# Every second piece of weights with its 16-bit groups of matmuls first

## The chip, the core and the metric

One NeuronCore of a Trainium2 chip runs the whole kernel. The metric is the device time of one execution in microseconds (us). Before the change three executions took 2743.44, 2739.66 and 2746.03 us, median 2743.44. One more execution was recorded by the hardware profiler. TensorE appears as PE (matmuls) and PEld (weight loads), VectorE as DVE, ScalarE as ACT, GpSimd as POOL, SyncE as SP; an engine's name with a q (SPq) is its queue of DMA issues.

## What is computed

A decoder block for 512 tokens with a model width of 2048, all in float32. The input is normalised and multiplied by one wide matrix; its columns feed a linear recurrence with matrix state (16 heads of 64), a sliding-window attention and two sets of gates. Both branches are projected, gated, added, projected again and added to the input. A gated feed-forward part with a short convolution follows. Cut to the lines that carry matrix products:

```
h = rms_norm(x, norm1_g)
z = h @ w_in                                  # 2048 x 9152
o_rw  = rwkv7_mix(token_shift(z[...]), ...)   # recurrence over 512 tokens
o_att = swa_attention(q, k, v, ...)
x = x + (sigmoid(zg_r) * (o_rw @ w_branch[:1024]) + sigmoid(zg_a) * (o_att @ w_branch[1024:])) @ w_out
h = rms_norm(x, norm2_g)
u = h @ w_up                                  # 2048 x 11264
x = x + (silu(gate) * val) @ w_down           # conv over 3 tokens in between; 5632 x 2048
```

## The kernel before

**Products in three groups.** [...] Weights arrive by DMA in a tile `raw`. ACT writes `whi`, the value rounded to the engine's 32-bit matmul type (float32r); DVE then writes `wlo = raw - whi` in bfloat16. The activations exist as `hi` (float32r) and `lo` (bfloat16) in the same way. A *piece* is one such converted tile of weights, and PE runs three groups of matmuls on it, always in this order: group 0 is hi times hi in the 32-bit type, group 1 is the upper half of `whi`, read as bfloat16 by `top()`, with the low activations, group 2 is `wlo` with bfloat16 activations. All three add into the same PSUM banks. Group 0 and 1 need `whi` from ACT, group 2 needs `wlo` from DVE, so `wlo` may be as late as two groups after a piece has begun.

**Three places do this.** `project` (line 273) serves the input projection and the branch projections: a piece is 128x512 weights, a group is 4 matmuls of 512 columns, and weights are the stationary operand. `steps_of` (line 1046) serves `w_out` and `w_down`, as seven products on half-size blocks: a piece is 128x1024, a group is 4 matmuls of 512 columns with the activations stationary; two pieces (`q` = 0 and 1) share one tile of activations. `Block.mm` (line 1185) serves `w_up`, seven products a column block as well: a piece is 128x1024, a group is 8 matmuls of 256 columns.

**Buffers.** The converted tiles rotate: 4 of each of `whi` and `wlo` in `project` (pool `hl`), 3 in the other two places (pool `hlp`). A `whi` buffer comes free when group 1 of its piece has ended, a `wlo` buffer when group 2 has ended, `raw` when DVE has made `wlo`. ACT and DVE each work through their own instructions in a fixed order, so an instruction that waits for a buffer holds up what stands behind it.

**What sets the order.** A scheduler places the instructions of the first half (input projection, attention, recurrence) from its own estimate of times; the recurrence's matmuls stand among those of `project` at set places of the list `stream` (`behind`). In `w_up` the order is written out (`steps`, `prep`, `run`): conversions run two pieces ahead of the matmuls, and `pin` keeps them as written.

Of the kernel before, what the change touches and what calls it, by code (L numbers as in the profile page):

```python
# [135 lines left out]
def block_kernel(ctx: ExitStack, tc: tile.TileContext, d: Dims, a: dict, out: bass.AP):  # L136
    nc = tc.nc
    act, dve, pool, pe, sync = nc.scalar, nc.vector, nc.gpsimd, nc.tensor, nc.sync
# [54 lines left out]
    def rsqrt_small(pl, ss, scale, eps, mx=None, tag="rq"):  # L193
        n = ss.shape[-1]
        tl = [pl.tile([P, 8], F32, name=f"{tag}{i}", tag=f"{tag}{i}", bufs=2)[:, :n] for i in range(3)]
        v, y, t = tl
        if mx is not None:
            dve.tensor_scalar(v, ss, mx, None, op0=ALU.max)
        else:
            dve.tensor_scalar(v, ss, scale, eps, op0=ALU.mult, op1=ALU.add)  # L200
        dve.tensor_scalar(t.bitcast(I32), v.bitcast(I32), 1, None, op0=ALU.logical_shift_right)
        dve.tensor_scalar(y.bitcast(I32), t.bitcast(I32), -1, 0x5F3759DF, op0=ALU.mult, op1=ALU.add)
        dve.tensor_scalar(v, v, -0.5, None, op0=ALU.mult)
        for _ in range(3):
            dve.tensor_tensor(t, y, y, op=ALU.mult)
            dve.tensor_tensor(t, t, v, op=ALU.mult)
            dve.scalar_tensor_tensor(y, t, 1.5, y, op0=ALU.add, op1=ALU.mult)
        return y

    pin = tc.keep_in_program_order  # L210
# [9 lines left out]
    def quarter(w, src, c):  # L220
        return sum_d[w][src][c] if isinstance(src, str) else a["w_" + w][src[0], src[1], 2 * c : 2 * c + 2]
# [21 lines left out]
        return lambda: pool.dma_start(dst, second, accum_op=ALU.add, max_dma_last_dim=4096)  # L243

    stream = []

    def top(x):
        x = x.bitcast(BF16)
        return x[(slice(None),) * (len(x.shape) - 1) + (slice(1, None, 2),)]
# [5 lines left out]
    def load_w(src):  # L255
        nk, ncol = src.shape[1:]
        n = nk * ncol
        raw = wp["raw"].tile([P, 512], F32, name="raw", tag="raw")[:, :n].rearrange("p (k c) -> p k c", c=ncol)
        wp["last"] = sync.dma_start(raw, src)
        hi = wp["hl"].tile([P, 512], F32R, name="whi", tag="whi")[:, :n].rearrange("p (k c) -> p k c", c=ncol)  # L260
        lo = wp["hl"].tile([P, 512], BF16, name="wlo", tag="wlo")[:, :n].rearrange("p (k c) -> p k c", c=ncol)
        act.activation(hi, raw, AF.Copy)  # L262
        dve.tensor_tensor(lo, raw, hi.bitcast(F32), op=ALU.subtract)  # L263
        wp["n"] += 1
        if wp["n"] in wp["after"]:
            wp["after"].pop(wp["n"])()
        elif wp["step"] == 3 and wp["n"] <= HELD:
            pass
        elif wp["n"] % wp["step"] == 0 or wp["n"] in extra:
            sums_along()()  # L270
        return hi, lo

    def project(acc, src, xhi, xlo, x16=None, pre=()):
        nk = src.shape[1]
        for k0 in range(0, nk, 4):
            n = min(4, nk - k0)
            whi, wlo = pre[k0 // 4] if k0 // 4 < len(pre) else load_w(src[:, k0 : k0 + n])
            ops = [[(whi[:, j], xhi[:, k0 + j]) for j in range(n)],
                   [(top(whi[:, j]), xlo[:, k0 + j]) for j in range(n)],
                   [(wlo[:, j], x16[:, k0 + j] if x16 is not None else top(xhi[:, k0 + j])) for j in range(n)]]  # L280
            for i, part in enumerate(ops):
                for j, (l, r) in enumerate(part):
                    stream.append(pe.matmul(acc, l, r, start=k0 + i + j == 0, stop=k0 + n == nk and i == 2 and j == n - 1))  # L283


    id16 = cstp.tile([P, P], F16, name="id16")
# [8 lines left out]
    if True:  # L295
# [39 lines left out]
        def ztile(c0):  # L335
            acc = accp.tile([P, S], F32, name="acc", tag="acc")
            project(acc, zt[c0], xhi, xlo, x16 if scaled else None, first.pop(c0, ()))
            return acc
# [5 lines left out]
        r = rsqrt_small(p0, ssum, 1.0 / d.D, RMS_EPS)  # L344
        spread = []
        with tc.tile_pool(name="x0_ps", bufs=1, space=PSUM) as ps0:
            ps = ps0.tile([P, S], F32, name="ps_r")
# [55 lines left out]
        with ExitStack() as pt:  # L403
# [4 lines left out]
            def small():  # L408
                return mps.tile([P, S], F32, name="mi", tag="mi")
# [53 lines left out]
            for t in range(1, NKV):  # L463
                for c0, then in ((d.c_ka, keys), (d.c_va, values)):
                    acc = ztile(c0 + t * P)
# [25 lines left out]
            for g in range(NHK):  # L491
# [7 lines left out]
                for n in range(NT):  # L499
                    ts = slice(n * P, (n + 1) * P)  # L500
                    k0 = 0 if n else BLK
                    nk = 2 * BLK - k0
# [29 lines left out]
                    for kb in kbs:  # L532
                        ps = small().rearrange("p (h c) -> p h c", c=P)
# [3 lines left out]
                    ps = small()  # L537
                    for kb in kbs:
                        for i in range(2):
                            pe.matmul(ps, vhl[:, n - 1 + kb, g].rearrange("p e c -> p (e c)"),  # L540
                                      phl[i][:, kb].rearrange("p h c -> p (h c)"),
                                      start=kb == kbs[0] and i == 0, stop=kb == kbs[-1] and i == 1)
                    ol = ap_.tile([HD, S], F32, name="ol", tag="ol", bufs=2)
                    act.activation(ol, ps[HD:P], AF.Copy)
                    ps, ol = (x[0:HD].rearrange("p (e j c) -> p e j c", e=2, c=P) for x in (ps, ol))
# [5 lines left out]
        with ExitStack() as pr:  # L551
# [30 lines left out]
            acc = ztile(d.c_wd)  # L582
# [5 lines left out]
            acc = ztile(d.c_ad)  # L588
# [3 lines left out]
            for i in range(NG):  # L592
                acc = ztile(d.c_gd + i * P)
# [354 lines left out]
    KH = NK // 2  # L948
# [27 lines left out]
    with ExitStack() as pbb:  # L976
# [5 lines left out]
        order = [(m + e, i) for m in range(0, NK - 4, 2) for i in (0, 1) for e in range(2)]  # L982
        order += [(m, i) for i in (1, 0) for m in range(NK - 4, NK)]
        g = {}
        for m, i in order:
            hi, lo, r0, n, gi = parts[i]
# [9 lines left out]
            acc = accp.tile([P, S], F32, name="acc", tag="acc")  # L996
# [36 lines left out]
    def raw_tile(nm="raw", n=6):  # L1033
        return rwp.tile([P, WC], F32, name=nm, tag=nm, bufs=n)

    def banks(pl, nm):
        return [[pl.tile([P, S], F32, name=f"{nm}{t}{q}") for q in range(NQW)] for t in range(NT // 2)]

    def fetch(w, i, c, pl, pin=free):

        hhi, hlo = (pl.tile([P, 2, TH], t, name=f"h{e}", tag=f"h{e}") for e, t in (("hi", F32R), ("lo", BF16)))
        hr = pl.tile([P, 2, TH], F32, name="hraw", tag="hraw")
        pin(sync.dma_start(hr, right_d[w][c][RIGHT_AT[PRODUCTS[i][3]]]))
        return lambda: split(hhi, hlo, hr, pin), hhi, hlo

    def steps_of(w, i, acc, c, pl, got=None):

        _, start, src, _, _ = PRODUCTS[i]
        make, hhi, hlo = got or fetch(w, i, c, pl)
        if not got:  # L1050
            make()
        for q in range(2):
            wr = raw_tile()
            sync.dma_start(wr, quarter(w, src, c)[q])
            whi, wlo = (hlp.tile([P, WC], t, name=f"w{e}", tag=f"w{e}") for e, t in (("hi", F32R), ("lo", BF16)))
            act.activation(whi, wr, AF.Copy)  # L1056
            dve.tensor_tensor(wlo, wr, whi.bitcast(F32), op=ALU.subtract)  # L1057
            fst, lst = start and c + q == 0, c == NB[w] - 1 and q == 1
            for j in range(3):
                for t in range(NT // 2):  # L1060
                    ts = slice(t * P, (t + 1) * P)
                    for e in range(NQW):
                        dst, es = acc[t][e], slice(e * S, (e + 1) * S)
                        l, r = ((hhi[:, q, ts], whi[:, es]), (hlo[:, q, ts], top(whi[:, es])), (top(hhi[:, q, ts]), wlo[:, es]))[j]
                        pe.matmul(dst, l, r, start=fst and j == 0, stop=lst and j == 2, skip_group_check=True)  # L1065

    def taken_out(i, acc, xr, scale, done):
        ci, tj, sign = PRODUCTS[i][4]
# [86 lines left out]
    class Block:  # L1155
# [29 lines left out]
        def mm(self, n):  # L1185
            if n == "P1":
                x = ups.tile([P, S], F32, name="X", tag="X")
                self.X = x[:, :TH]
                self.Z = x[:, TH:] if self.f < NPRE else upy.tile([P, S], F32, name="Z", tag="Y")[:, :TH]
            if n == "P7":  # L1190
                self.Y = upy.tile([P, S], F32, name="Y", tag="Y")[:, :TH]
            into = {"P2": "Z", "P7": "Y", "Q4": "Y"}.get(n, "X")
            ps = getattr(self, "Z" if self.apart and n in ("P5", "P3") else into)
            start = n in ("P1", "P7") or n == "P2" and self.f >= NPRE or n == "P5" and self.apart
            whi, wlo = (x.rearrange("p (k c) -> p k c", c=P) for x in self.hl.pop(n))
            xh, xl = bq[{"P1": "b11", "P2": "b21", "P7": "t3", "P6": "t2", "P5": "t1", "Q4": "t4", "P3": "b22"}[n]]
            for i in range(3):
                for k in range(KH):
                    l, r = ((whi[:, k], xh[:, k]), (top(whi[:, k]), xl[:, k]), (wlo[:, k], top(xh[:, k])))[i]
                    pin(pe.matmul(ps, l, r, start=start and k + i == 0, stop=k == KH - 1 and i == 2, skip_group_check=True))  # L1200

        def out(self, n):
            if n == "P7":
# [74 lines left out]
    queue, order = [], {x: i for i, x in enumerate(steps)}  # L1278
# [65 lines left out]
    with tc.tile_pool(name="sqp", bufs=1, side="right", reuse_waits="tile") as sqp:  # L1344
        yx = ExitStack()
        py = yx.enter_context(tc.tile_pool(name="psY", bufs=1, space=PSUM, side="right", reuse_waits="tile"))
        acc = {"X": banks(px, "X"), "Y": banks(py, "Y")}
# [116 lines left out]
    with ExitStack() as pd:  # L1464
        pxy = pd.enter_context(tc.tile_pool(name="psD", bufs=1, space=PSUM, reuse_waits="tile"))
        acc = {n: banks(pxy, n) for n in "YX"}
# [94 lines left out]
```

## Time and profile before

| what | value |
|---|---|
| three executions | 2739.66 to 2746.03 us, median 2743.44 |
| the profiled execution | 2737.99 us, span of the core 2736.2 us |
| PE busy in the span | 2678.0 us |
| DVE, ACT, POOL busy | 1993.9, 1345.1, 231.3 us |
| granted TensorE clock | 0.999 |
| input projection, attention, recurrence | from 0 to about 1300 us |
| `w_out` | about 1300 to 1450 us |
| `w_up` | about 1448 to 2310 us |
| `w_down` | about 2300 to 2736 us |

The stages are told apart by the lines of the matmuls: line 283 is `project`, line 1065 `steps_of`, line 1200 `Block.mm`. In a row of the groups the columns are line, engine, operation, what is written and read, shapes, count, then busy time and the mean length of one in ns, then idle time before it and who ended that. In a row of the timeline they are start in us, length in us, engine, line, operation, operands and count; rows of neighbours of one kind are merged, so a row's length runs from the first one's start to the last one's end. Matmuls of a stream overlap in such rows: each record is longer than the distance to the next start.

### The profile page before, as it was taken

To read this page: it belongs to the slowest core of one execution; us is meant where nothing else is said; L and a number is where in the kernel's file an instruction comes from. 1 tells how busy PE (TensorE), PEld (TensorE's weight loads), DVE (VectorE), ACT (ScalarE), POOL (GpSimd) and SP (SyncE) were. 2 spreads that over 40 slices of the span, in tenths; PEclk is the share of its full clock that TensorE was granted. 3 is DMA by queue.
4 is the path that set the end of the run, shared out by engine and by line. 5 is a ranking of instruction groups with operands and counts; after the bars stand their busy time and mean duration, and the time that the engine had idled before them with its cause. 6 is when DMAs were issued, how large, how long until landed. Compare 5 with 4: busy or idle time off the path is not lost.

```text
span 2736.2 us, 45737 instructions
## 1 busy us (share of the span) xinstructions
PE 2678.0 (98%) x17227; PEld 1832.8 (67%) x17410; DVE 1993.9 (73%) x3476; ACT 1345.1 (49%) x2261; POOL 231.3 (8%) x308
## 2 busy tenths in 40 slices
PE   8999999999999999999999999999999999999999
PEld 4555566666666665555558889999999998555554
DVE  6787777877787775455678788888888888555655
ACT  6445445544544543322466555555555555444443
POOL 0001111111111001011000111101111110000000
PEclk9999999999999999999999999999999999999999
DMA  6557788779878767888785889888899888877775
GB/s 238 157 152 199 209 217 214 205 196 232 212 198 213 186 178 210 257 244 292 252 275 170 234 231 250 251 235 241 244 250 246 236 238 280 295 241 245 259 256 181
DMA packets 228333, 623.80 MB, mean 228 GB/s; under 512 B 24960, under 2 KB 45072, under 8 KB 227088
## 3 DMA queue, kind: packets, MB, share of 16 engines
q1 hardware_dynamic: 159552, 445.23, 49.4%
q0 software_dynamic: 37216, 136.33, 25.6%
q10 hardware_dynamic: 31344, 39.31, 4.1%
q8 instruction: 136, 2.23, 0.3%
q14 instruction: 85, 0.70, 0.1%
HBM read 571.16 MB, written 191.18 MB: 279 GB/s over the span
## 4 chain that ended last, share of the span: by engine, by line
PE 81%; DVE 10%; DMA 4%; ACT 2%; issue 2%; SPq 0%; DVEq 0%; ACTq 0%
PE acc L283 26%; PE X L1200 16%; PE X L1065 11%; PE Y L1065 9%; PE Y L1200 8%; PE Z L1200 4%; DVE wlo L263 2%; PE psS L833 1%; PE psG L824 1%; DMA rsb<-rsd 1%; DVE wlo L1183 1%; PE bulk L809 1%; DMA raw<-in_w_dn_dram 1%; DMA raw<-in_w_z_dram 1%; PE bulk L761 1%
## 5 line engine op out<-in xcount | busy, mean ns | idle before, releaser
L1057 DVE TENSOR_TENSOR wlo<-raw,whi 128x1024 bf16<-128x1024 f32 x210 | 256.7, 1225 | 192.2 <-ACT whi L1056 192.0
L283 PE MATMUL acc<-xhi,whi 128*128 128x512 f32 x1152 | 376.8, 441 | 10.9 <-ACT whi L262 10.4
L262 ACT ACTIVATE whi<-raw 128x512 fp32r<-128x512 f32 x352 | 220.1, 629 | 313.0 <-PE acc L283 251.3
L1056 ACT ACTIVATE whi<-raw 128x1024 fp32r<-128x1024 f32 x210 | 222.2, 1060 | 278.2 <-PE X L1065 146.3
L263 DVE TENSOR_TENSOR wlo<-raw,whi 128x512 bf16<-128x512 f32 x352 | 239.7, 688 | 97.7 <-ACT whi L262 59.9
L283 PE MATMUL acc<-xlo,whi 128*128 128x512 bf16 x1080 | 301.2, 383 | 4.0 <-issue 0.5
L283 PE MATMUL acc<-xlo,wlo 128*128 128x512 bf16 x1028 | 279.5, 379 | 2.1
L1183 DVE TENSOR_TENSOR wlo<-raw,whi 128x1024 bf16<-128x1024 f32 x184 | 224.8, 1223 | 72.5 <-ACT whi L1181 71.8
L1200 PEld LDWEIGHTS <-wlo 128*128 128x128 bf16 x2464 | 237.4, 96 | 39.5
L283 PEld LDWEIGHTS acc<-xhi,whi 128*128 128x128 f32 x1152 | 211.6, 190 | 65.2 <-ACT whi L262 11.5
L1181 ACT ACTIVATE whi<-a 128x1024 fp32r<-128x1024 f32 x124 | 131.0, 1056 | 228.3 <-DVE a L1176 209.8
L1200 PEld LDWEIGHTS <-whi 128*128 128x128 bf16 x2464 | 216.8, 98 | 34.7
L283 PEld LDWEIGHTS <-wlo 128*128 128x128 bf16 x1408 | 135.4, 98 | 150.3 <-issue 5.2
L283 PEld LDWEIGHTS <-whi 128*128 128x128 bf16 x1408 | 111.8, 100 | 159.4 <-issue 95.5
L1183 DVE TENSOR_TENSOR wlo<-a,whi 128x1024 bf16<-128x1024 f32 x124 | 152.0, 1225 | 64.2 <-ACT whi L1181 62.9
L1181 ACT ACTIVATE whi<-raw 128x1024 fp32r<-128x1024 f32 x184 | 192.4, 1047 | 3.3 <-PE X L1200 1.6
L1200 PE MATMUL X<-b,whi 128*128 128x256 f32 (+1 forms) x1472 | 192.1, 283 | 0.8 <-ACT whi L1181 0.3
L1200 PE MATMUL X<-t,whi 128*128 128x256 f32 (+1 forms) x1408 | 183.8, 283 | 3.2 <-ACT u L1227 2.5
L1200 PE MATMUL Y<-t,whi 128*128 128x256 f32 (+1 forms) x1408 | 183.8, 283 | 0.5 <-DVE u L1229 0.5
L1065 PE MATMUL X<-whi,hhi 128*128 128x512 f32 x480 | 153.3, 441 | 1.6 <-ACT whi L1056 1.6
L1065 PEld LDWEIGHTS <-hhi 128*128 128x128 bf16 x840 | 81.5, 97 | 103.7
L1251 DVE SCALAR_TENSOR_TENSOR c<-u,par,c 128x512 f32<-128x512 f32 x176 | 131.5, 747 | 14.1 <-ACT c L1248 13.9
(389 smaller groups left out, 4584.2 us busy)
## 6 DMA issues: line engine op xcount, KB each, us to landing
raw<-in_w_up_dram SPq DMA_DIRECT2D x170, 512.0 KB
raw<-in_w_z_dram SPq DMA_DIRECT2D x288, 256.0 KB
s_dn<-in_w_dn_dram POOLq DMA_DIRECT2D x88, 512.0 KB, 7.5
raw<-s_dn SPq DMA_DIRECT2D x88, 512.0 KB
raw<-in_w_up_dram POOLq DMA_DIRECT2D x80, 512.0 KB, 8.7
raw<-in_w_dn_dram SPq DMA_DIRECT2D x66, 512.0 KB
s_dn<-in_w_dn_dram SPq DMA_DIRECT2D x44, 512.0 KB
s_dn<-s_dn SPq DMA_DIRECT2D x44, 512.0 KB
```

The lines of the kernel that those rows point to most:

```text
L262: act.activation(hi, raw, AF.Copy)
L263: dve.tensor_tensor(lo, raw, hi.bitcast(F32), op=ALU.subtract)
L283: stream.append(pe.matmul(acc, l, r, start=k0 + i + j == 0, stop=k0 + n == nk and i == 2 and j == n - 1))
L761: ins = pe.matmul(ps[:, n], wt[:, 0, n], both(n), start=True, stop=False)
L809: pin(pe.transpose(ps[:, e, q], X[:, e, 2 * q : 2 * q + 2].rearrange("p n c -> p (n c)"), id16))
L1056: act.activation(whi, wr, AF.Copy)
L1057: dve.tensor_tensor(wlo, wr, whi.bitcast(F32), op=ALU.subtract)
L1065: pe.matmul(dst, l, r, start=fst and j == 0, stop=lst and j == 2, skip_group_check=True)
L1181: pin(act.activation(hi, t, AF.Copy))
L1183: return lambda: pin(dve.tensor_tensor(lo, t, hi.bitcast(F32), op=ALU.subtract))
L1200: pin(pe.matmul(ps, l, r, start=start and k + i == 0, stop=k == KH - 1 and i == 2, skip_group_check=True))
L1251: pin(dve.scalar_tensor_tensor(t, u[:, i, j + 1 : j + 1 + S], cw[:, j + 1, ci : ci + 1], t, op0=ALU.mult, op1=ALU.add))
```

## The change

A pair of orders, `turns`, is defined. Even pieces keep groups 0, 1, 2; odd pieces run 1, 2, 0. What counts as odd is the second and fourth piece of a projection in `project`, the piece `q` = 1 in `steps_of`, and every second step of the written order in `Block.mm`. [...] No instruction is added or taken away.

```diff
     stream = []
+    turns = ((0, 1, 2), (1, 2, 0))
...
-            for i, part in enumerate(ops):
-                for j, (l, r) in enumerate(part):
-                    stream.append(pe.matmul(acc, l, r, start=k0 + i + j == 0, stop=k0 + n == nk and i == 2 and j == n - 1))
+            ops = [x for i in turns[k0 // 4 % 2] for x in ops[i]]
+            for j, (l, r) in enumerate(ops):
+                stream.append(pe.matmul(acc, l, r, start=k0 + j == 0, stop=k0 + n == nk and j == len(ops) - 1))
...
-            for j in range(3):
+            order = turns[q]
+            for j in order:
...
-                        pe.matmul(dst, l, r, start=fst and j == 0, stop=lst and j == 2, skip_group_check=True)
+                        pe.matmul(dst, l, r, start=fst and j == order[0], stop=lst and j == order[2],
+                                  skip_group_check=True)
...
-            for i in range(3):
+            way = turns[order[self.f, n] % 2]
+            for i in way:
...
-                    pin(pe.matmul(ps, l, r, start=start and k + i == 0, stop=k == KH - 1 and i == 2, skip_group_check=True))
+                    pin(pe.matmul(ps, l, r, start=start and k == 0 and i == way[0],
+                                  stop=k == KH - 1 and i == way[2], skip_group_check=True))
```

On PE, in `w_out`, the boundary from a piece `q` = 0 to its piece `q` = 1 stood like this before (a 16-bit matmul has a separate LDWEIGHTS row, a 32-bit one carries its load with it; X_13661 to X_13664 are the four banks):

```order
L1065 LDWEIGHTS hhi
L1065 MATMUL X_13664<-wlo,hhi 128x512
L1065 MATMUL X_13661<-whi,hhi 128x512
L1065 MATMUL X_13662<-whi,hhi 128x512
L1065 MATMUL X_13663<-whi,hhi 128x512
L1065 MATMUL X_13664<-whi,hhi 128x512
L1065 LDWEIGHTS hlo
L1065 MATMUL X_13661<-whi,hlo 128x512
```

Of the change, PE at the end of the piece `q` = 1 and the start of the next piece:

```order
L1067 LDWEIGHTS hhi
L1067 MATMUL X_13664<-wlo,hhi 128x512
L1067 MATMUL X_13661<-whi,hhi 128x512
L1067 MATMUL X_13662<-whi,hhi 128x512
L1067 MATMUL X_13663<-whi,hhi 128x512
L1067 MATMUL X_13664<-whi,hhi 128x512
L1067 MATMUL X_13661<-whi,hhi 128x512
L1067 MATMUL X_13662<-whi,hhi 128x512
L1067 MATMUL X_13663<-whi,hhi 128x512
L1067 MATMUL X_13664<-whi,hhi 128x512
L1067 LDWEIGHTS hlo
L1067 MATMUL X_13661<-whi,hlo 128x512
```

Before, each run of four 32-bit matmuls stood between 16-bit ones; now the eight of two pieces stand together, and the sixteen 16-bit ones of the next two likewise.

In the stage of the recurrence the scheduler also moves conversions on ACT. Before, in the part that sets up a pair of heads (AI, XIW, BX and W are tiles of the recurrence, L262 is the conversion to `whi`):

```order
L216 ACTIVATE AI<-at__5436 128x512
L262 ACTIVATE whi<-raw 128x512
L216 ACTIVATE XIW<-tt 128x256
L729 COPY BX<-tt 64x4x64
L745 ACTIVATE W_2877<-bulk 128x4x2x64
L216 ACTIVATE AI<-at__5454 128x512
```

The same place on ACT now (line numbers one higher):

```order
L216 ACTIVATE AI<-at__5436 128x512
L746 ACTIVATE W_2877<-bulk 128x4x2x64
L216 ACTIVATE XIW<-tt 128x256
L730 COPY BX<-tt 64x4x64
L216 ACTIVATE AI<-at__5454 128x512
L746 ACTIVATE W_2877<-bulk 128x4x2x64
L756 ACTIVATE SV<-bulk 64x4x64 x4
L263 ACTIVATE whi<-raw 128x512
```

The conversion stands behind six instructions of the recurrence that it used to stand ahead of. On PE itself the recurrence's matmuls keep their places among those of `project` but for shifts of one to six matmuls in a few of them.

## The prediction, made before the changed kernel ran

> **What bounds the kernel now.** I read the shares of the engines first, then the chain of work that ended last, then the busy time by stretch.
>
> ```profile
> PE 2678.0 (98%) x17227; PEld 1832.8 (67%) x17410; DVE 1993.9 (73%) x3476; ACT 1345.1 (49%) x2261; POOL 231.3 (8%) x308
> PE 81%; DVE 10%; DMA 4%; ACT 2%; issue 2%; SPq 0%; DVEq 0%; ACTq 0%
> 1580.00:1900.00 320.00, 319.76 (x2790) 289.00 (x2789) 262.26 (x318) 170.24 (x235) 36.06 (x42) 1.00 0.89 242
> 1900.00:2320.00 420.00, 419.87 (x3630) 376.96 (x3629) 345.77 (x421) 224.34 (x309) 45.87 (x55) 1.00 0.89 246
> ```
>
> PE is busy for 98% of the span and holds 81% of the last chain; in the two stretches of `w_up` (columns: stretch, length, then busy time of PE, PEld, DVE, ACT, POOL, the granted clock, the DMA share) it has no idle time at all at a full clock. Whatever shortens PE's own sequence shortens the kernel, and the question is what the sequence of types costs PE. DVE is the second engine, 82% busy in both stretches, so a demand for earlier results from DVE must be looked at too.
>
> **What the change removes: changes of type.** Before, every piece has one change from 32-bit to 16-bit matmuls and one back. After, two pieces share one of each. The number of pieces follows from the weight loads of group 2, of which a piece has 4, 4 and 8:
>
> ```profile
> L283 PEld LDWEIGHTS <-wlo 128*128 128x128 bf16 x1408 | 135.4, 98 | 150.3 <-issue 5.2
> L1065 PEld LDWEIGHTS <-hhi 128*128 128x128 bf16 x840 | 81.5, 97 | 103.7
> L1200 PEld LDWEIGHTS <-wlo 128*128 128x128 bf16 x2464 | 237.4, 96 | 39.5
> ```
>
> 1408/4 = 352, 840/4 = 210 and 2464/8 = 308 pieces: 176, 105 and 154 pairs, 435 changes each way less. What is one round (there and back) worth? In `w_down` the timeline shows whole pieces, and narrow windows show three matmuls of a group without the first:
>
> ```profile
> 2602.72 1.28 PE L1065 MATMUL X<-whi,hhi 128*128 128x512 f32 x4
> ...
> 2605.43 1.28 PE L1065 MATMUL X<-whi,hhi 128*128 128x512 f32 x4
> 2606.55 0.56 PEld L1065 LDWEIGHTS <-hlo 128*128 128x128 bf16 x4 [0.27 <-issue]
> 2607.25 0.75 PEld L1065 LDWEIGHTS <-hhi 128*128 128x128 bf16 x4
> 2607.47 1.02 PE L1065 MATMUL X<-wlo,hhi 128*128 128x512 bf16 x4
> 2700.70 0.86 PE L1065 MATMUL X<-whi,hhi 128*128 128x512 f32 x3
> 2701.64 0.84 PE L1065 MATMUL X<-whi,hlo 128*128 128x512 bf16 x3
> L1065 PE MATMUL X<-whi,hlo x4: 387/387/398, 2701.4 to 2702.1; 128*128 128x512 bf16 x4
> L1065 PE MATMUL X<-whi,hhi x3: 393/393/397, 2700.7 to 2701.2; 128*128 128x512 f32 x3
> L1065 PE MATMUL X<-wlo,hhi x3: 377/377/378, 2702.3 to 2702.8; 128*128 128x512 bf16 x3
> ```
>
> The last three rows give shortest, median and longest record in ns. A merged row is (n-1) steps plus one record, so the steps are (0.86-0.397)/2 = 0.231 us for group 0, (0.84-0.387)/2 = 0.227 for group 1, (1.02-0.378)/3 = 0.214 for group 2. Four of each are 2.688 us. The period is 2605.43-2602.72 = 2.71. The rest, **0.02 us**, belongs to the two changes. Where it falls is visible: the first 16-bit record after a 32-bit group is 398 ns long and its fellows 387, and the first loads of `hlo` come after 0.27 us without a load, where those of `hhi` come with no gap. Rounding leaves the 0.02 open to about 0.01 to 0.03; the 11 ns of the longer record alone are the lower end.
>
> The other two places are read alike. In `project` both 16-bit groups read their moving operand without stride and differ only in which comes behind the 32-bit group:
>
> ```profile
> L283 PE MATMUL acc<-xlo,whi 128*128 128x512 bf16 x1080 | 301.2, 383 | 4.0 <-issue 0.5
> L283 PE MATMUL acc<-xlo,wlo 128*128 128x512 bf16 x1028 | 279.5, 379 | 2.1
> ```
>
> 383 against 379 ns in the mean is 4 x 4 = 16 ns a group. For `w_up`:
>
> ```profile
> 2014.29 5.49 PE X L1200 x48
> 2033.51 5.49 PE X L1200 x48
> 2102.14 0.99 PE L1200 MATMUL Y<-t,whi 128*128 128x256 f32 x7
> 2100.46 0.82 PE L1200 MATMUL X<-b,whi 128*128 128x256 bf16 x6
> 2101.11 1.07 PE L1200 MATMUL X<-b,wlo 128*128 128x256 bf16 x8
> L1200 PE MATMUL X<-b,whi x9: 272/273/286, 2100.1 to 2101.0; 128*128 128x256 bf16 x8, 128*128 128x256 f32 x1
> L1200 PE MATMUL Y<-t,whi x9: 278/282/367, 2101.9 to 2103.0; 128*128 128x256 f32 x8, 128*128 128x256 bf16 x1
> L1200 PE MATMUL X<-b,wlo x8: 275/275/276, 2101.1 to 2101.9; 128*128 128x256 bf16 x8
> ```
>
> The two rows of the chain are the same step of two column blocks, seven pieces apart: 19.22/7 = 2.746 us a piece. The steps are (0.99-0.282)/6 = 0.118, (0.82-0.273)/5 = 0.109 and (1.07-0.275)/7 = 0.114; eight of each are 2.728. The rest is 0.018 us.
>
> Together: 176 x 0.016 + 105 x 0.020 + 154 x 0.018 = 2.8 + 2.1 + 2.8 = **7.7 us** less on PE. With 0.011 and 0.030 for each of the 435, the bounds are 4.8 and 13. I take the middle, since three separate readings lie at 16 to 20 ns. That runs of eight or sixteen 32-bit matmuls keep their step isn't shown anywhere in this trace; within runs of eight in `w_up` the step shows no drift, and I count nothing for it.
>
> [...]
>
> **What it moves: `wlo` is due one group earlier.** In an odd piece group 2 comes second. In `w_down` there is ample room:
>
> ```profile
> 2604.96 1.06 ACT L1056 ACTIVATE whi<-raw 128x1024 fp32r<-128x1024 f32 x1 [1.65 <-PE X L1065]
> 2606.05 1.23 DVE L1057 TENSOR_TENSOR wlo<-raw,whi 128x1024 bf16<-128x1024 f32 x1 [1.49 <-ACT whi L1056]
> ```
>
> With three buffers this conversion, released by the piece begun at 2602.72, serves the third one after it, begun at 2602.72 + 3 x 2.71 = 2610.85. `wlo` is ready at 2607.28. An odd piece would ask for it at about 2610.85 + 4 x 0.227 = 2611.76: 4.5 us of slack. The `whi` buffer of an odd piece is also freed one group (0.9 us) later, which takes 0.9 of that and leaves 3.6; `raw`, and the next load on SP behind it, follow by the same 0.9 us in every second piece, where six buffers lie ahead. `project` has four buffers. Both cost nothing.
>
> `w_up` is the tight place. Its tightest steady piece and the one at the beginning:
>
> ```profile
> 2071.42 1.23 DVE L1183 TENSOR_TENSOR wlo<-raw,whi 128x1024 bf16<-128x1024 f32 x1 [1.65 <-ACT whi L1181]
> 2072.76 0.77 PEld L1200 LDWEIGHTS <-whi 128*128 128x128 bf16 x8
> 1487.33 1.22 DVE L1183 TENSOR_TENSOR wlo<-raw,whi 128x1024 bf16<-128x1024 f32 x1
> 1488.12 0.77 PEld L1200 LDWEIGHTS <-whi 128*128 128x128 bf16 x8
> 1488.90 0.89 PEld L1200 LDWEIGHTS <-wlo 128*128 128x128 bf16 x8
> ```
>
> Group 1 starts where an odd piece will want `wlo`. At 2072 `wlo` is ready at 2072.65, 0.11 us ahead; at 1487 it is ready at 1488.55, in time for the old place (1488.90) and 0.43 late for 1488.12. Two more pieces about 1544 and 1553 would be some 0.15 late. That is **0.7 us** lost; behind the waiting matmul only PE's own queue stands, and DVE, which works ahead, loses nothing. Another 0.2 us I take off for the pieces of the first 60 us and of 1480 to 1580, where PE waits for others anyway.
>
> **Sum.** 7.7 - 0.7 - 0.2 = 6.8 us. The profiled execution took 2737.99, which becomes 2731.2. It lies 5.5 us below the median of the three runs, and the gain is per instruction and not of that execution, so from the median: 2743.4 - 6.8 = **2736.6 us**.
>
> **Rivals.**
> *No gain to be seen* (0.24): the 16 to 20 ns could belong to the beginning of the group and not to the change of type, and wait at the new boundaries between 16-bit groups of two pieces, or be given back there. For it: the rest is small beside the rounding. Against it: the second 16-bit group of each piece begins without such a loss though its operands change too. Time 2743, with the tight pieces 2744.
> *Slower, by ACT's queue in the recurrence* (0.08): `whi` of an odd piece is held four more matmuls, 4 x 0.216 = 0.86 us. ACT waits for such buffers already, and a recurrence instruction that stands behind a waiting conversion starts late by the same time; PE then waits at the place where its result is due.
>
> ```profile
> ACT whi L262 <- PE acc L283: 251.3, 172, 5.5
> 610.45 0.63 ACT L262 ACTIVATE whi<-raw 128x512 fp32r<-128x512 f32 x1 [0.22 <-PE acc L283]
> PE psG L824 <- DVE SV L837: 4.5, 4, 1.6
> ```
>
> The eight pairs of heads hold 8 x 6 tiles of 4 pieces, 96 of them odd. If a quarter of these held up the recurrence, 24 x 0.86 = 20.6 us would outweigh the gain: 2743.4 - 7.7 + 20.6 = 2756. It decides from nine such pieces on. Against it: the order shows these conversions moved behind the recurrence's instructions, and PE waits only 4.5 us in all at its worst place there.
> *A large gain* (0.04): the whole load of 96 ns is exposed at each change. 435 x 0.096 = 42 us, 2702. The period of 2.71 us speaks against it.
>
> **Numbers.** The forecast has 0.64, and of that 0.10 for a gain that comes out under 0.2% (5.5 us, about what a measurement of this kernel can tell from no change). So faster 0.54 + 0.04 = 0.58, same 0.10 + 0.24 = 0.34, slower 0.08. The range reaches from 2743.4 - 13 - 2 (spread of the runs) = 2728 to 2743.4 + 2.6, the highest run seen, 2746.
>
> **What would show it.** In the profile after: the gap of 0.27 us before `hlo` loads appears once in two pieces; two pieces of `w_down` take 5.40 us and not 5.42; the mean record of `xlo,whi` in `project` falls from 383 toward 381; waits of PE for DVE's `wlo` appear near 1487 and sum to under 1 us. If the 32-bit step in runs of eight is longer than 0.231, or PE's waits for the recurrence grow by several us, the forecast is wrong.

## The result, and the profile after

| kernel | runs | median | lowest to highest |
|---|---|---|---|
| before | 6 | 2741.55 us | 2736.13 to 2746.03 |
| changed | 6 | 2726.99 us | 2722.78 to 2727.36 |

The ratio of the times is 0.9951, with a 95% interval of 0.994 to 0.9963. That is 13.4 us less (10.1 to 16.4), about twice the forecast of 6.8, and the median lies 1 us under the lower end of the range. The range was worked out from 2743.4 us; as a ratio its lower end is 2728/2743.4 = 0.9944, and 0.9951 lies inside. The profiled execution took 2727.0 us with a span of 2725.2, against 2737.99 and 2736.2 before.

The page of the changed kernel, first the shares of the engines, then from the busy time by stretch the second half of `w_up`:

```profile
PE 2679.8 (98%) x17410; PEld 1855.7 (68%) x17410; DVE 1993.9 (73%) x3476; ACT 1342.3 (49%) x2261; POOL 231.5 (8%) x308
1900.00:2320.00 420.00, 420.00 (x3610) 376.75 (x3609) 346.18 (x423) 224.62 (x309) 46.11 (x55) 1.00 0.90 250
```

PE is the bound as before. Its busy time has even grown by 1.8 us, while the span lost 11: the trace of before lacks 183 matmul records (17227 against 17410 loads), so the busy time can't be compared, only periods can.

A pair of pieces in `w_down`, from the timeline of after, two rows of PE and two of its loads:

```profile
2523.99 2.20 PE L1067 MATMUL Y<-whi,hhi 128*128 128x512 f32 x8
...
2529.39 2.20 PE L1067 MATMUL Y<-whi,hhi 128*128 128x512 f32 x8
...
2597.71 0.76 PEld L1067 LDWEIGHTS <-hlo 128*128 128x128 bf16 x4
...
2601.53 0.57 PEld L1067 LDWEIGHTS <-hlo 128*128 128x128 bf16 x4 [0.27 <-issue]
```

The pair takes 5.40 us, and the 0.27 us without a load stands ahead of one of its two `hlo` groups and not of the other: both as forecast. The chain of work that ended last gives the pair more sharply, since it counts 264 matmuls, or 22 pieces, as one entry; from the timeline of before, two rows 51 pieces apart stand for the old period:

```profile
2363.47 59.33 PE Y L1067 x264
2422.80 59.33 PE X L1067 x264
```

```profile
2521.43 1.28 PE L1065 MATMUL Y<-whi,hhi 128*128 128x512 f32 x4
...
2659.63 1.28 PE L1065 MATMUL Y<-whi,hhi 128*128 128x512 f32 x4
```

59.33/11 = 5.394 us a pair after, 2 x 138.20/51 = 5.420 before: 0.026 us saved in a pair. In `w_up` two column blocks, 14 pieces, lie between these rows of the chain, of before and of after:

```profile
2014.29 5.49 PE X L1200 x48
...
2052.74 5.49 PE X L1200 x48
```

```profile
2008.08 5.48 PE X L1204 x48
...
2046.44 5.48 PE X L1204 x48
```

38.45 became 38.36, or 0.013 us a pair. The waits of PE for `wlo` in the whole execution of after (columns: who waits for whom, us in total, times, longest):

```profile
PE acc L284 <- DVE wlo L264: 0.8, 1, 0.8
...
PE Y L1204 <- DVE wlo L1186: 0.4, 1, 0.4
...
PE Z L1204 <- DVE wlo L1186: 0.2, 1, 0.2
PE X L1204 <- DVE wlo L1186: 0.2, 1, 0.2
```

The forecast had three late `wlo` of 0.43, 0.15 and 0.15 us in `w_up`; there they are. So far the steps hold, and they add up to 105 x 0.026 + 154 x 0.013 - 0.8 = 3.9 us in the two stages after the recurrence, where the forecast had 2.1 + 2.8 - 0.7 = 4.2. What it didn't have lies in the first stage. DVE makes one `vz` for each pair of heads; the groups by line, cut to the seventh and eighth of them, give first and last start, of before and of after:

```profile
L568 DVE SCALAR_TENSOR_TENSOR vz<-acc,omu,zpad x2: 751/751/751, 841.6 to 937.0; 128x512 f32<-128x512 f32 x2
```

```profile
L569 DVE SCALAR_TENSOR_TENSOR vz<-acc,omu,zpad x2: 750/750/750, 834.9 to 929.4; 128x512 f32<-128x512 f32 x2
```

A pair of heads takes 94.5 us where it took 95.4. It holds 24 pieces of `project`, so 12 pairs; at the forecast's 0.016 they explain 0.2 us of the 0.9, at 0.026 they explain 0.3. At this rate eight pairs of heads would make 7 us. The traces show a little less, since other pairs are lengthened by single waits that differ between executions; first and last start of all eight, of before and of after:

```profile
L568 DVE SCALAR_TENSOR_TENSOR vz<-acc,omu,zpad x8: 746/751/751, 311.1 to 937.0; 128x512 f32<-128x512 f32 x8
```

```profile
L569 DVE SCALAR_TENSOR_TENSOR vz<-acc,omu,zpad x8: 745/750/752, 308.8 to 929.4; 128x512 f32<-128x512 f32 x8
```

625.9 us became 620.6, or 5.3 less in these two executions. Behind the recurrence `project` runs without it, and there the change of type is seen alone. Two rows that lie two pieces apart, from the timeline of PE before and after:

```profile
1181.01 1.28 PE L283 MATMUL acc<-ahi,whi 128*128 128x512 f32 x4
...
1186.43 1.29 PE L283 MATMUL acc<-rhi,whi 128*128 128x512 f32 x4
```

```profile
1184.03 1.28 PE L284 MATMUL acc<-rhi,whi 128*128 128x512 f32 x4
...
1189.41 2.20 PE L284 MATMUL acc<-ahi,whi 128*128 128x512 f32 x8
```

A pair of pieces takes 5.38 to 5.39 us where it took 5.42: 0.03 us, almost twice the forecast's 0.016. The 352 - 192 = 160 pieces outside the pairs of heads are 80 pairs, and 80 x 0.03 = 2.4 us is an estimate of what the types bring there.

In the pairs of heads the order of ACT and DVE has changed, as the order of the change showed. One place, from the timeline: before,

```profile
549.89 0.43 DVE L777 TENSOR_TENSOR tt<-bulk,tt 128x256 f32<-128x256 f32 x1
...
550.23 0.69 DVE L263 TENSOR_TENSOR wlo<-raw,whi 128x512 bf16<-128x512 f32 x1
...
550.95 0.43 DVE L813 COPY BT<-bulk 64x512 f16<-64x512 f16 x1
...
551.41 0.43 DVE L787 TENSOR_TENSOR tt<-tt,cst 128x256 f32<-128x256 f32 x1
...
552.53 0.42 DVE L217 TENSOR_TENSOR XIW<-tt,XIW 128x256 f16<-128x256 f32 x1
...
553.01 0.20 PE L761 MATMUL bulk<-XIW,BT 128*128 128x64 f16 x1 [0.25 <-DVE XIW L217]
```

and the same step after (line numbers one higher):

```profile
546.00 0.42 DVE L778 TENSOR_TENSOR tt<-bulk,tt 128x256 f32<-128x256 f32 x1
...
546.46 0.43 DVE L788 TENSOR_TENSOR tt<-tt,cst 128x256 f32<-128x256 f32 x1
...
548.05 0.41 DVE L217 TENSOR_TENSOR XIW<-tt,XIW 128x256 f16<-128x256 f32 x1
548.38 1.40 DVE L264 TENSOR_TENSOR wlo<-raw,whi 128x512 bf16<-128x512 f32 x2
...
548.83 0.19 PE L762 MATMUL bulk<-XIW,BT 128*128 128x64 f16 x1
```

The sum `tt` (L777) goes through a mask (L787) into `XIW`, for which PE waits. Before, `tt` is ready at 550.32, but the conversion to `wlo` and a copy `BT` stand ahead of the mask on DVE, which starts at 551.41; `XIW` is late, and PE waits 0.25 us. After, the mask follows at once, two conversions stand together behind `XIW`, and PE does not wait. From the sum to PE's matmul it took 3.12 us before and 2.83 after. That is one place in one pair of heads. Over the whole execution PE's waits for `XIW` at this line hardly fall: 1.9 us in 8 waits before, 1.8 in 6 after. Another wait of PE is gone altogether; before,

```profile
PE bulk L764 <- DVE AI L217: 1.4, 5, 0.3
```

and after there is none at that line, although PE's own order around it is the same. And ACT's conversions in `project`, which before waited 251.3 us for PE to free a buffer, wait 157.6 us after. Two places show ready work that stands behind what was placed ahead of it. On DVE it is the mask above, which starts 1.09 us after `tt` is ready. On ACT, before, the recurrence's `UV` stands behind a conversion that waits for a buffer:

```profile
1057.48 0.39 PE L827 MATMUL psU<-GY,BX 128*128 128x128 f32 x2
...
1057.68 0.63 ACT L262 ACTIVATE whi<-raw 128x512 fp32r<-128x512 f32 x1 [3.26 <-PE acc L283]
...
1058.22 0.20 ACT L828 ACTIVATE UV<-psU 64x64 f32<-64x64 f32 x1
```

The records of `psU` end at 1057.87, and `UV` starts 0.35 us later. Why the scheduler may put conversions later follows from the change: the `whi` of an odd piece is in use until the piece's end and not only until group 1, so the buffer that a conversion asks for comes free one group later.

### The profile page after: what moved, and what is told of

Read it like the earlier page. It is cut to its first block, busy times and chain, and to the rows that moved or that the text cites. A ratio compares the mean times of both kernels' runs of the same rounds, so it can differ in the third digit from the quotient of the medians.

```text
span 2725.2 us, 45733 instructions
## 1 busy us (share of the span) xinstructions
PE 2679.8 (98%) x17410; PEld 1855.7 (68%) x17410; DVE 1993.9 (73%) x3476; ACT 1342.3 (49%) x2261; POOL 231.5 (8%) x308
## 4 chain that ended last, share of the span: by engine, by line
PE 47%; DVE 3%; issue 1%; ACT 1%; DMA 0%; ACTq 0%; DVEq 0%
PE X L1204 15%; PE X L1067 11%; PE Y L1067 9%; PE Y L1204 8%; PE Z L1204 3%; DVE wlo L1186 1%; ACT whi L1184 1%; DVE c L1256 0%; DVE a L1179 0%; PE ps_t L1133 0%; DMA raw<-in_w_up_dram 0%; ACT c L1253 0%; DVE t L1153 0%; PE ps_t L1135 0%; DVE u L1236 0%
## 5 line engine op out<-in xcount | busy, mean ns | idle before, releaser
L284 PE MATMUL acc<-xhi,whi 128*128 128x512 f32 x1152 | 351.5, 427 | 10.6 <-ACT whi L263 10.4
L263 ACT ACTIVATE whi<-raw 128x512 fp32r<-128x512 f32 x352 | 218.6, 626 | 252.9 <-PE acc L284 157.6
L284 PE MATMUL acc<-xlo,whi 128*128 128x512 bf16 x1152 | 312.6, 383 | 0.7 <-DVE xlo L314 0.4
L284 PE MATMUL acc<-xlo,wlo 128*128 128x512 bf16 x1072 | 289.0, 380 | 0.8 <-DVE wlo L264 0.8
L1204 PEld LDWEIGHTS <-whi 128*128 128x128 bf16 x2464 | 227.8, 98 | 36.2 <-ACT whi L1184 2.7
L284 PEld LDWEIGHTS <-whi 128*128 128x128 bf16 x1408 | 123.9, 100 | 151.6 <-issue 47.2
L1204 PE MATMUL X<-t,whi 128*128 128x256 bf16 (+1 forms) x1408 | 185.6, 280 | 3.2 <-ACT u L1232 2.7
L1067 PEld LDWEIGHTS <-hlo 128*128 128x128 bf16 x840 | 73.1, 97 | 107.8 <-issue 27.8
```

The source lines that it names most:

```text
L284: stream.append(pe.matmul(acc, l, r, start=k0 + j == 0, stop=k0 + n == nk and j == len(ops) - 1))
L1067: pe.matmul(dst, l, r, start=fst and j == order[0], stop=lst and j == order[2], skip_group_check=True)
L1204: pin(pe.matmul(ps, l, r, start=start and k == 0 and i == way[0], stop=k == KH - 1 and i == way[2], skip_group_check=True))
```

## The experiments

Two causes stood against each other for the stage of `project`: fewer changes of type on PE, or conversions that stand later in the queues of ACT and DVE. Each run has its own runs of before beside it, and the microseconds below are the ratio's share of those medians (2737 to 2739 us). The ratio is not the quotient of the two medians: for the change in `project` alone the medians lie 6.9 us apart and not 9.3, with `whi` held and the types as before 7.0 and not 8.8.

**The change in one place at a time.** `project` alone:

```diff
-            order = turns[q]
+            order = turns[0]
...
-            way = turns[order[self.f, n] % 2]
+            way = turns[0]
```

> The new order in project alone (176 pairs), the old one elsewhere. Theory 'types': the gain is the change of type that two pieces now share. After its trace a pair costs 0.030 us less in undisturbed stretches, so -5.3 us by the pairs; the rest of the 9.9 us that this stage gained in the profile of the change is chance of one execution: ratio about 0.998. Theory 'recurrence': the moved conversions of ACT and DVE also free the recurrence of waits, and the whole 9.9 us come back in the timed runs: ratio about 0.9964.

Measured: 2731.7 us, ratio 0.9966 (0.9953 to 0.9979), 9.3 us less. `project` holds most of the gain, over three times the 2.8 us that the forecast gave it.

`steps_of` alone (the other two with `turns[0]`):

> The new order in steps_of alone (105 pairs). 'Types': 105 x 0.030 = -3.2 us, ratio 0.9989, a pair of pieces in the middle of w_down takes 5.39 us and not 5.42; the project stage ends where it ended before, within 2 us. If the 4 us lost at the start of w_out come from the new order itself, they show here too and the total is about +1; if they come of a DMA that landed late in one execution, they are absent.

Measured: 2740.44 us, ratio 1.0006 (0.9996 to 1.0017): no gain.

`Block.mm` alone:

> The new order in Block.mm alone (154 pairs). 'Types': the trace of the change shows 0.013 us a pair in the steady part, since runs of sixteen 32-bit matmuls go at 0.120 us and not 0.118, so -2.0 us, less 1 us of waits for wlo at the start of w_up: -1 us, ratio 0.9996. If the drift within the longer run were chance of one trace, the step stays at 0.118 and the pair gains 0.02 or more: -3 us.

Measured: 2736.87 us, ratio 0.9994 (0.9981 to 1.0008): nothing that can be told from no change. Both together, `project` as before:

```diff
-            ops = [x for i in turns[k0 // 4 % 2] for x in ops[i]]
+            ops = [x for i in turns[0] for x in ops[i]]
```

> The new order in steps_of and Block.mm, project as before. By the steps of the profile after (0.030 us a pair in steps_of, 0.013 in w_up): 105 x 0.030 + 154 x 0.013 = 5.2 us, less 1.6 us of waits for wlo: 3.6 us faster (ratio 0.9987). By the sum of the two runs that had one of them each: 0 (1.000). By the forecast's terms: 4.2 us (0.9985). Project's end as before, w_down's 15 pieces at 40.43 us instead of 40.65, w_up's 28 pieces at 76.72 instead of 76.91.

Measured: 2733.1 us, ratio 0.9981 (0.9972 to 0.9991), 5.2 us less (2.5 to 7.7). The chain of this kernel has an entry of the change's length in `w_down`:

```profile
2371.74 59.33 PE Y L1067 x264
```

So the two later stages bring some 5 us together, and with the 9.3 of `project` the change's 13.4 is accounted for within the intervals. How the 5 us split is not settled: the run of `steps_of` alone showed none of its part, and its interval ends at 1.1 us less, where its pieces should save 2.7. In its profile the pieces do save that, 5.39 us a pair in `w_down` (from 2524.03 to 2529.42); but PE waits 4.3 us there for one `whi` at 2328, and the granted clock is 0.66 from 2326 to 2336. Before, a wait of 1.6 us stood near that place, at full clock. Whether the timed runs had the longer wait is not known.

**As many changes of type as before.** Odd pieces run 1, 0, 2, so each keeps one change there and one back, and `whi` is free at the same point as before:

```diff
-    turns = ((0, 1, 2), (1, 2, 0))
+    turns = ((0, 1, 2), (1, 0, 2))
```

> Odd pieces run groups 1, 0, 2 everywhere: pieces still begin with different groups, buffers are still held longer and the scheduler still moves conversions, but two pieces have as many changes of type as before (32 to 16 twice). 'Types': within 2 us of the kernel before (ratio 0.9993 to 1.0007), a pair in w_down 5.42 us. 'Recurrence' or any theory by which the moved conversions bring the gain: 4 us or more faster.

Measured: 2738.04 us, ratio 0.9994 (0.9981 to 1.0008). That the order differs by itself brings nothing that can be told from no change. Taken alone, this run would have spoken for the types; but it leaves both causes out, since the conversions hardly move in it either: 5 of 2259 instructions of ACT and 6 of 3476 of DVE, told by operation and tile, stand at another place than before; in the change it is 354 and 419. That is why the next one was needed.

**`whi` held, types as before.** In `project` alone, odd pieces run 2, 0, 1: as many changes of type as before, but `whi` is in use until the piece's end, as in the change:

```diff
-    turns = ((0, 1, 2), (1, 2, 0))
+    turns = ((0, 1, 2), (2, 0, 1))
```

> Project only: odd pieces run group 2 first, then 0, then 1; every other stage as before. A pair of pieces has the same two rounds of type changes as before, but whi of an odd piece is held to the end of the piece, as in the change. Theory A (the gain of the project stage beyond the pairs' own 0.030 us comes from the conversions moved behind the recurrence's instructions): the undisturbed head-pair period falls from 95.5 to about 94.8, the kernel is 4 to 5 us faster than before (ratio about 0.9983), about half of the 9.3 us of the run with the new order in project alone. Theory B (all of the gain is type changes): 0, ratio 1.000. Theory C (all of it is the moved conversions): 9 us, 0.9967.

Measured: 2730.09 us, ratio 0.9968 (0.995 to 0.9985), 8.8 us less (4.1 to 13.7). The theory of types alone falls. The middle is nearly all of what `project` brings; the interval still reaches down to the 4 to 5 us of the theory that gave the conversions half of it. Up to 1.8 us may belong to this order itself, since behind the recurrence its pair of pieces takes 5.41 us and not 5.42 (about 0.01 in 176 pairs). Its `vz`, and those of the run with 1, 0, 2:

```profile
L569 DVE SCALAR_TENSOR_TENSOR vz<-acc,omu,zpad x2: 750/751/752, 840.1 to 934.7; 128x512 f32<-128x512 f32 x2
```

```profile
L569 DVE SCALAR_TENSOR_TENSOR vz<-acc,omu,zpad x2: 751/751/751, 842.0 to 937.5; 128x512 f32<-128x512 f32 x2
```

94.6 us a pair of heads where `whi` is held, 95.5 where it is not, with the same number of rounds of types in both. The change itself had 94.5: in these pairs of heads the types bring about 0.1 us of the 0.9. The profiled execution of the run with `whi` held took 2737.95 us, 8 above its median, and other pairs in it are longer: from the first `vz` to the last it took 625.0 us, hardly less than before. So the 8.8 us rest on the timed runs, and the profile adds the undisturbed pair alone.

**Conversions later, and every piece's order untouched.** Before, with one buffer of `whi` less in `project`; the groups of every piece run as before:

```diff
-        hi = wp["hl"].tile([P, 512], F32R, name="whi", tag="whi")[...]
+        hi = wp["hl"].tile([P, 512], F32R, name="whi", tag="whi", bufs=3)[...]
```

> Before, with three buffers instead of four for whi in project and the order of the matmuls as before everywhere: conversions become free to run later, and so stand later in the queues of ACT and DVE, with no change of type taken away. If moving the conversions behind the recurrence's instructions is what gains in project: head-pair period below 95.5 us (as far as 94.6), 2 to 7 us faster than before (ratio 0.9975 to 0.9993); if PE then waits for late conversions, the gain is eaten and the ratio is 1.000 or above with new waits of PE for whi or wlo. If type changes are the whole gain: 1.000, period 95.5.

Measured: 2730.74 us, ratio 0.9972 (0.9962 to 0.9983), 7.7 us less (4.7 to 10.4). A kernel with a buffer *less* is faster, and that without any change of type taken away.

```profile
L568 DVE SCALAR_TENSOR_TENSOR vz<-acc,omu,zpad x2: 750/751/752, 833.4 to 928.3; 128x512 f32<-128x512 f32 x2
```

94.9 us a pair of heads. How long ACT's conversions wait for PE to free a buffer, 251.3 us before, tells the kernels apart in the same way. In order, the run with 2, 0, 1, this one, and the one with 1, 0, 2 that gained nothing:

```profile
ACT whi L263 <- PE acc L284: 183.6, 149, 8.6
```

```profile
ACT whi L262 <- PE acc L283: 196.2, 171, 3.0
```

```profile
ACT whi L263 <- PE acc L284: 257.7, 169, 5.0
```

PE's wait for `AI` goes with them: it is gone in the first two and stands in the third as it stood before,

```profile
PE bulk L765 <- DVE AI L217: 1.4, 5, 0.3
```

Together, the run with 2, 0, 1 and this one show that the gain in `project` beyond the types comes from the order that the scheduler makes when a buffer of `whi` comes free later. That the conversions are what matters in this order is argued from the waits and not shown by a run of its own: the matmuls of the recurrence also change their places among those of `project`. Counted by PE's weight loads, 417 of them move in the change and in the run with 2, 0, 1, by up to six places; 1488 move in this one, by up to ten; with 1, 0, 2 none does. No run moved the conversions alone. Nor was the 0.9 us itemised: the wait for `AI` holds some 0.3 of it, in five pairs of heads.

**All of `whi` held.** The change, but with `project` at 2, 1, 0 and 0, 2, 1: as few changes of type as in the change, and `whi` in use until the end of every piece:

```diff
+    held = ((2, 1, 0), (0, 2, 1))
...
-            ops = [x for i in turns[k0 // 4 % 2] for x in ops[i]]
+            ops = [x for i in held[k0 // 4 % 2] for x in ops[i]]
```

> The change, but project's pieces run 2, 1, 0 and 0, 2, 1: as few type changes as in the change, and whi held to the end of every piece instead of every second one. If the moved conversions gain in proportion to how many are moved: 3 to 7 us faster than the change (2716 to 2720, ratio to before about 0.993); if the places that waited are already free in the change: as the change, 0.995; if wlo, wanted first in the even pieces, comes late: slower than the change, with waits of PE for wlo at line 284 or 285.

Measured: 2739.26 us, ratio 0.9998 (0.9987 to 1.001): the gain is gone. The first of PE's waits:

```profile
PE acc L285 <- DVE wlo L265: 18.6, 7, 8.7
```

With group 2 first, an even piece asks for `wlo` at its start, and PE waits 18.6 us for `wlo` and 0.2 for `whi` in `project`, where the change waited 0.8 and 10.6: 7.4 us more together, over half of what this run loses against the change. A pair of heads takes 95.2 us, so most of the gain there is gone as well; why was not followed up.

**`wlo` one more group earlier.** Odd pieces run 2, 1, 0 everywhere:

```diff
-    turns = ((0, 1, 2), (1, 2, 0))
+    turns = ((0, 1, 2), (2, 1, 0))
```

> Odd pieces run 2, 1, 0 everywhere: as few type changes as in the change, wlo wanted one more group earlier (0.87 us), whi of odd pieces held to the end. If the pairs and the held whi are the gain, project gains as in the change (its end near 1282). In w_up, wlo comes late in the tight pieces: by the slack that the trace of before shows (under 0.5 us in some 25 odd pieces) PE waits 8 to 12 us for wlo there, and the kernel stands at 0.998 to 0.9995 of before instead of 0.995. If wlo's lateness costs nothing: 0.995.

Measured: 2732.19 us, ratio 0.9982 (0.9973 to 0.9992), 4.9 us less. PE's waits in `w_up`:

```profile
PE X L1204 <- DVE wlo L1186: 4.5, 8, 1.5
PE Z L1204 <- DVE wlo L1186: 2.6, 1, 2.6
PE Y L1204 <- DVE wlo L1186: 1.3, 1, 1.3
```

8.4 us where the change had 0.8, within the 8 to 12 expected: it costs most of the difference to the change. The slack of `wlo` in `w_up` reaches to the place at which the change asks for it, and hardly further.

**One more round of types in each piece.** Before, with group 0 of `steps_of` cut in two around group 1:

```diff
-            for j in range(3):
-                for t in range(NT // 2):
+            for j, tt in ((0, (0,)), (1, (0, 1)), (0, (1,)), (2, (0, 1))):
+                for t in tt:
```

> Before, with group 0 of each of the 210 pieces of steps_of cut into two halves around group 1 (half of group 0, group 1, the other half, group 2): one more round of type changes in every piece, 210 in all. At the forecast's 0.020 us a round: +4.2 us (ratio 1.0015); at 0.030 as read from the profile after: +6.3 us (1.0023); if a change costs nothing by itself: 0. In the undisturbed stretch of w_down 15 pieces take 40.65 us before and should take 40.95 at 0.020, 41.1 at 0.030.

Measured: 2742.91 us, ratio 1.0015 (1.0001 to 1.003), 4.1 us more (0.3 to 8.2). The chain in `w_down`:

```profile
2442.61 60.06 PE X L1066 x264
```

60.06/22 = 2.730 us a piece against 2.710: a round there and back costs 0.020 us, the forecast's figure to the last digit.

**Both kernels once more.** The changed kernel:

> The changed kernel once more, for a second profile. If the wait of 2 us at the beginning of w_out and the half-speed matmuls behind it are chance (a DMA landing late), they are absent or smaller here; if the new order makes them, they are there again with about 4 us. The end of project should again lie about 10 us earlier than in the profile before (1291.6), and the median at 0.995 of before.

Measured: 2722.66 us, ratio 0.9943 (0.9923 to 0.9964). Its seventh and eighth `vz` start 94.5 us apart again. The kernel before:

> The kernel before once more, for a second profile: the head-pair period of 95.5 us and the end of project near 1290 us should be there again if they belong to the kernel and not to one execution; ratio 1.000.

Measured: 2736.73 us, ratio 0.9996 (0.9981 to 1.0011), and 95.5 us from `vz` to `vz`.

The change with three buffers of `whi` besides was not run; whether the two add up is open.

## Why the prediction was right in its sign and half the size

*PE's own sequence as the bound.* Right in the stages behind the recurrence: what they lost is seen in PE's periods. In the stage of the recurrence the larger part came through the order of what PE waits for.

*A round of type changes.* Right in size. `steps_of`: 0.020 forecast, 0.020 measured by adding a round, 0.026 saved by removing one. `w_up`: 0.018 forecast, 0.013 measured; why runs of sixteen save less than runs of eight was not isolated, and the forecast had left open whether long runs keep their step. The added round took 0.020 us a piece (2.730 against 2.710); the first rival, no gain, falls with it.

*`project` at 176 x 0.016 = 2.8 us.* About right for the types, too small as the account of that stage. Where the recurrence's matmuls stand between the pieces, the types bring about 0.1 us a pair of heads, by the runs with and without a held `whi`; that is 8 x 0.1 = 0.8 us there. Outside, 80 pairs of pieces at 0.03 bring some 2.4. The two make about 3.2 us, an estimate, of the stage's 9.3; that it comes near the 2.8 is luck, for 0.016 was too small for the pieces outside and too large for the others. The sign I had watched for, the mean record of `xlo,whi`, stayed at 383 ns.

*`wlo` due one group earlier, 0.7 us.* Right in `w_up`: 0.8 us at three places. `project` added one wait of 0.8 for `wlo` that the forecast had at nothing.

*`whi` held four matmuls longer, "both cost nothing".* **This is the step that failed.** I counted a later release only as slack used up, saw that it can hold up ACT's queue, and priced that as the rival on the slower side. The release has a second effect: the scheduler, told of it, places the first half anew, with the conversions later, behind instructions of the recurrence. I had the order of the change before me, with a conversion moved behind six such instructions, and used it only as an argument against the rival, not as a gain of its own. The two runs that keep every round of types show 8.8 us (4.1 to 13.7) and 7.7 (4.7 to 10.4) for it, in the middle more than all of the forecast; in the change itself it is the rest of the 9.3 that the types leave, some 6 us by the estimate above. The stage's 9.3 and the 5.2 of the two others make 14.5 us, within the 10.1 to 16.4 of the change. The rival on the slower side did not come about: PE's wait for `SV`, 4.5 us in all, did not grow but fell to 2.7.

*The large gain of 42 us.* Nothing of it was seen.

## What to carry over

When a change alters how long a buffer is held, look at where the scheduler then puts the instruction that refills it, and at who stands behind it: here `UV` started 0.35 us late on ACT behind a conversion that had waited for its buffer, and the mask 1.09 us late on DVE behind a conversion and a copy. More buffers were not better here: one fewer of `whi` gained 7.7 us. And a run that keeps one cause must remove the other: the order 1, 0, 2 left out both and would have confirmed the wrong one. A run that lets the scheduler place things anew moves more than what it is meant to move, so compare the order of every engine before reading it as a run of one cause.

## What was not expected of the hardware

In the profile after, a conversion for `w_out` came late, and PE stood idle once; then it ran at half pace. The timeline of PE, and busy time by stretch with the granted clock as the third figure from the end:

```profile
1295.53 1.41 PE L1067 MATMUL X<-whi,hhi 128*128 128x512 f32 x4 [2.17 <-ACT whi L1057]
1296.73 1.93 PE L1067 MATMUL X<-whi,hlo 128*128 128x512 bf16 x4
1298.46 1.67 PE L1067 MATMUL X<-wlo,hhi 128*128 128x512 bf16 x4
1299.97 1.06 PE L1067 MATMUL X<-whi,hlo 128*128 128x512 bf16 x4
1300.87 1.02 PE L1067 MATMUL X<-wlo,hhi 128*128 128x512 bf16 x4
```

```profile
1296.70:1299.90 3.20, 3.20 (x9) 1.16 (x9) 2.30 (x3) 1.73 (x2) 0.00 (x0) 0.52 0.84 264
1300.00:1310.00 10.00, 10.00 (x46) 5.63 (x45) 6.74 (x9) 4.21 (x5) 0.00 (x0) 1.00 0.80 263
```

Behind a wait of 2.17 us the granted clock was 0.52 for 3.2 us: the four matmuls of `hlo` took 1.73 us to the start of the next group, where the next `hlo` group, at a clock of 1.00, took 0.90. The place cost more than the wait. Such a wait is not always followed by a lower clock: before, a wait of 2.52 us in `w_up` at 1549.53 left the clock at 1.00 (from 1549.60 to 1552.80), and in the second profile of the kernel before the same wait at 1546.75 was followed by a clock of 0.60 (from 1547.40 to 1550.60). What decides was not isolated. In the second profile of the changed kernel PE did not wait at that place, so the new order doesn't make the stall.
